# Reading x first and summing the first conditioning blocks on TensorE in a hybrid decoder layer

## The chip, the cores and the metric

The kernel runs on one core of one Trainium2 chip. The metric is the device time of one execution in microseconds. It covers the whole layer: all weights are read from HBM in float32, and all products are formed on the chip.

## What is computed

One decoder layer on 512 tokens of width 2048. A conditioning vector `c` gives six modulation vectors; the first two of them (shift and scale of the mixer's norm) are what the change concerns. Cut to that part, the reference is:

```python
c_act = jax.nn.silu(c)
mod = c_act @ w_ada[l] + b_ada[l]                  # 2048 x 12288 weights
sh_m, sc_m, gt_m, sh_f, sc_f, gt_f = jnp.split(mod[:, None, :], 6, axis=-1)
h = rmsnorm(x, pre_mix_norm[l]) * (1.0 + sc_m) + sh_m
proj = h @ w_in[l]                                 # 512 x 2048 by 2048 x 8208
o_hg = hgrn2_group(proj[..., :HG_COLS], ...)       # gated recurrences, chunks of 64
o_gdn = gdn_group(proj[..., HG_COLS:], ...)
y = concatenate([o_hg, o_gdn]) @ w_out[l]
x = x + gt_m * rmsnorm(y, post_mix_norm[l])
h = rmsnorm(x, pre_ffn_norm[l]) * (1.0 + sc_f) + sh_f
y = square(relu(h @ w_ff1[l])) @ w_ff2[l]
x = x + gt_f * rmsnorm(y, post_ffn_norm[l])
```

## The kernel before, in words

**Stages.** The program has a start stage, a mixer stage, an output projection and a feed-forward stage. In all of them a float32 product is formed as three matmuls of rounded parts (`mm3`): high part by high part, high by low, low by high. ScalarE makes the high part of a weight tile (L197) and VectorE (sometimes Pool) the low part (L199).

**The start stage.** The model width of 2048 is cut into 16 blocks of 128 rows, here called blocks 0 to 15 (`kt`). For each block the stage needs a scale and a shift vector of 128 numbers. Each is a sum over the 2048 entries of `c_act`, times a column of `w_ada`. The needed part of `w_ada` (33.5 MB) is packed as 128 tiles of 128 x 512 (256 KB), two to a slot: one of the scale, one of the shift. `GROUPS` says which blocks share a slot: before, blocks 0 and 1 are groups by themselves (four slots each), and the other blocks go in pairs (eight slots each). There are 64 slots.

A slot's tile holds, for w = 128 columns, four row sets side by side; for w = 256, two. `ada_vector` (L440) multiplies each row set by one entry of `c_act` per partition and adds it to a sum, one VectorE pass a row set. `ada_pool` does the same for the shift tile: ScalarE scales the row sets in place (L449), and Pool adds the whole tile to a sum of 128 x 512 (L451). In group 0 VectorE does both tiles (`NV = 1`). When a group's slots are through, TensorE sums over the partitions by `column_sum` (ones as the moving operand, two matmuls of 64 columns each), and VectorE forms the scale `sc1` and shift `shm` (L845 to L847).

**The norm of x.** x is loaded in eight transfers of 512 KB (L798), after the first four slots (`X_AT = 4`). ScalarE squares each half row block and sums it (L633), VectorE and Pool form the reciprocal root (L426, L427: a `pow` on Pool), TensorE spreads it over the partitions (`spread`), and VectorE copies it into `R1`.

**From blocks to matmuls.** `mod_thread` takes the groups in order. For each block it transposes x on TensorE (L342; block 0 beforehand), multiplies by scale and `R1` on VectorE (L858, `ht`), and writes the high part `hH` (ScalarE) and the low part `hL` (VectorE L863; from block 4 on, for even blocks, Pool L868). A token ("mod", block) then releases the matmuls of that block. `CUTS` orders these as units of eight weight tiles: `(first block, number of blocks, from, to)` over the list of 16 column blocks (two heads of each kind). A unit of two blocks covers four column blocks, a unit of four covers two. The first five column blocks accumulate in PSUM banks of their own; the others are partial sums that VectorE adds into SBUF after each unit (L705).

**What sets the order.** In the start stage the queues of TensorE, ScalarE and SyncE are written out in the order of a small planner (`run`). It keeps a modelled clock: each matmul costs its modelled time, each load 0.73 or 1.46 us on a modelled DMA clock (`on_load`), a thread yields the time that it means to wait, and while all threads wait, the next projection matmuls are emitted (`fill_thread`). The planner does not model VectorE or Pool; their order is the framework's. `AHEAD = 7` slots are loaded ahead. The slot tiles rotate over 14 tiles that are not yet otherwise used and `NADA` more. A weight tile is loaded three units ahead.

**Masks.** `masks` builds on Pool the constant masks for the later recurrences, one of six steps for each group that `mod_thread` begins.

Of the kernel before, what the change touches and what calls it, by code (L numbers as in the profile page):

```python
# [8 lines left out]
F32 = mybir.dt.float32  # L9
# [4 lines left out]
ALU = mybir.AluOpType  # L14

P = 128
NADA = 2
ADV = 0.17
LP0 = 7
LP1 = 23  # L20
# [1 line left out]
LATE = 20  # L22
AHEAD = 7
X_IN = 3.0
X_AT = 4
W_AT2 = 8
W_AT = 4
NLAST = 5
SLACK = 1.57
SLACK1 = 1.0  # L30
NV = 1
PJ = 3
LOOK = 6
T = 512
D = 2048
KT = D // P
# [10 lines left out]
    ("g", 0, (C_GQ, C_GK, C_GV, C_GG)), ("g", 1, (C_GQ, C_GK, C_GV, C_GG)),  # L47
    ("h", 0, (C_HF, C_HQ, C_HI, C_HG)), ("h", 1, (C_HF, C_HQ, C_HI, C_HG))))
START_BLOCKS = G0 + H0 + G1 + H1
CUTS = [(0, 2, 0, 16), (2, 2, 0, 16), (4, 2, 0, 8), (6, 2, 0, 8), (4, 4, 8, 16),  # L50
        (8, 4, 0, 8), (12, 4, 0, 8), (8, 4, 8, 16), (12, 4, 8, 16)]
START_UNITS = [(k0, nk, START_BLOCKS[i : i + 8 // nk])
               for k0, nk, lo, hi in CUTS for i in range(lo, hi, 8 // nk)]
IN1_COLS = [cc + h * P for h in range(2, NH) for cc in (C_GK, C_GQ, C_GV, C_HF, C_HQ, C_HI, C_GG, C_HG)]

GROUPS = [(0,), (1,)] + [(k, k + 1) for k in range(2, KT, 2)]
SLOTS = [(g, j) for g, kts in enumerate(GROUPS) for j in range(4 * len(kts))]
ADA_REST = (4, 3, 2, 5)


def by_tiles(name, a):

    import numpy as np

    if name == "w_ada":
        w = a[0].reshape(P, KT, -1)
        out = []
        for g, j in SLOTS:
            n = len(GROUPS[g]) * P
            nr = 512 // n  # L70
            for seg in (1, 0):
                c0 = seg * D + GROUPS[g][0] * P
                out.append(w[:, nr * j : nr * (j + 1), c0 : c0 + n].reshape(P, 512))
        for seg in ADA_REST:
            for cb in range(4):
                for r in range(KT):
                    out.append(w[:, r, seg * D + cb * 512 : seg * D + (cb + 1) * 512])
        return np.stack(out)
    if name == "w_in":
        w = a[0].reshape(KT, P, -1).transpose(1, 0, 2)  # L80
        out = []
        for k0, nk, bls in START_UNITS:
            out.append(np.concatenate([w[:, k0 : k0 + nk, cc + h * P : cc + (h + 1) * P] for _, h, cc in bls], 1))
        for col in IN1_COLS:
            for hf in range(2):
                out.append(w[:, 8 * hf : 8 * (hf + 1), col : col + P])
        return np.concatenate([t.reshape(-1) for t in out] + [w[:, :, C_AB : C_AB + 16].reshape(-1)])
    if name == "w_ff1":
        return a[0].reshape(4, 4, P, DFF // 256, 256).transpose(3, 0, 2, 1, 4).reshape(-1, P, 1024)
    if name in ("w_out", "w_ff2"):  # L90
        return a[0].reshape(-1, 2, P, 4, 512).transpose(0, 3, 2, 1, 4).reshape(-1, P, 1024)
    return a
# [143 lines left out]
def hybrid_layer_kernel(  # L236
# [7 lines left out]
    nc = tc.nc  # L244
    PSUM = bass.MemoryType.PSUM
    xf = x[0]
# [105 lines left out]
    ones = const.tile([P, P], F32, name="ones")  # L352
# [3 lines left out]
    mhalf = const.tile([P, 16], F32, name="mhalf")  # L356
# [49 lines left out]
    c2 = const.tile([P, KT], F32, name="c2")  # L406
# [14 lines left out]
    tl = const.tile([P, NCH, NH], F32, name="tl")  # L421
    fold = const.tile([32, 16], F32, name="fold")

    def rsqrt_to(dst, src, scale, eps):
        n = src.shape[1]
        nc.vector.tensor_scalar(out=dst, in0=src, scalar1=scale, scalar2=eps, op0=ALU.mult, op1=ALU.add)  # L426
        nc.gpsimd.tensor_tensor(out=dst, in0=dst, in1=mhalf[:, :n], op=ALU.pow)  # L427

    def ada_load(alloc, seg, cb, r):
        a = alloc(f"ada{seg}_{cb}_{r}")  # L430
# [3 lines left out]
    def ada_vector(a, ncol, r0, nr, acc, first):  # L434
        for r in range(nr):
            av, cv = a[:, r * ncol : (r + 1) * ncol], c2[:, r0 + r : r0 + r + 1]
            if first and r == 0:
                nc.vector.tensor_scalar(out=acc, in0=av, scalar1=cv, scalar2=None, op0=ALU.mult)
            else:
                nc.vector.scalar_tensor_tensor(out=acc, in0=av, scalar=cv, in1=acc, op0=ALU.mult, op1=ALU.add)  # L440
# [12 lines left out]
    def column_sum(ps, i, a, w, start=True, stop=True):  # L453
        for g in range(2):
            s = slice(64 * g, 64 * (g + 1))
            mm(ps[s, i, : w.shape[1]], a[:, s], w, start, stop, cost=0.08)
# [91 lines left out]
    def sm(name):  # L548
        return bank("wh", name)
# [215 lines left out]
    def on_load(us):  # L765
        dma[0] = max(dma[0], clock[0]) + us
# [16 lines left out]
    xarr = []  # L783
    masking = masks()

    def ada_thread():
        nl = 0
        for i, (g, j) in enumerate(SLOTS):
            w = len(GROUPS[g]) * P
            nr = 512 // w  # L790
            while nl < min(len(SLOTS), i + 1 + AHEAD):
                ada_slot(nl)
                nl += 1
                if nl == X_AT:
                    for tok in range(4):
                        for hf in range(2):
                            hs = slice(hf * 1024, (hf + 1) * 1024)
                            nc.sync.dma_start(out=xn4[:, tok, hs], in_=xf[tok * P : (tok + 1) * P, hs])  # L798
                            on_load(1.46)
                            xarr.append(dma[0])  # L800
                    tokens.add(("xload", 0))
                if nl == W_AT:
                    ws._load()
                if nl == LATE:
                    late_loads()
                if nl == W_AT2:
                    for _ in range(2):
                        ws._load()
            at, t = arrive.pop(i)
            yield max(0.0, at + (ADV if g > 0 else 1.0) - clock[0])  # L810
            if j == 0:
                sums[g] = [sp.tile([P, n], F32, tag=f"asum{n}", name=f"asum{n}_{g}", bufs=2)
                           for n in (256, 512)]
            ada_vector(t[0], w, nr * j, nr, sums[g][0][:, :w], j == 0)
            if g < NV:
                ada_vector(t[1], w, nr * j, nr, sums[g][1][:, :w], j == 0)
            else:
                ada_pool(t[1], w, nr * j, nr, sums[g][1], j == 0)
            if j == 4 * len(GROUPS[g]) - 1:
                tokens.add(("ada", g))  # L820
# [5 lines left out]
    def mod_thread():  # L826
        for g, kts in enumerate(GROUPS):
            w = len(kts) * P
            if g > 0:
                next(masking, None)  # L830
            if g == 3:
                late_consts()
            yield "ada", g
            yield 2.0 if g else 0.5
            n = len(kts)
            asc, ash = sums.pop(g)
            pc = sm(f"pc{g}").rearrange("p (k n) -> p k n", n=64)
            nr = 1 if g < NV else 512 // w
            for i in range(n):
                column_sum(pc, i, asc[:, i * P : (i + 1) * P], ones[:, :64])  # L840
                for r in range(nr):
                    column_sum(pc, n + i, ash[:, r * w + i * P : r * w + (i + 1) * P], ones[:, :64],
                               r == 0, r == nr - 1)
            ks = slice(kts[0], kts[0] + n)
            nc.vector.tensor_tensor(out=sc1[:, ks], in0=pc[:, 0:n, 0], in1=b_scm[:, ks], op=ALU.add)  # L845
            nc.vector.tensor_tensor(out=sc1[:, ks], in0=sc1[:, ks], in1=w_pm[:, ks], op=ALU.mult)
            nc.vector.tensor_tensor(out=shm[:, ks], in0=pc[:, n : 2 * n, 0], in1=b_shm[:, ks], op=ALU.add)  # L847
            if g == 0:
                yield "x", 0
            for kt in kts:  # L850
                if kt in early:
                    ps = early[kt]
                else:
                    yield 0.5
                    ps = sm(f"pt{kt}")
                    x_transposes(ps, kt)
                ht = mt("ht", f"ht{kt}", 2)
                nc.vector.scalar_tensor_tensor(out=ht, in0=ps, scalar=sc1[:, kt : kt + 1], in1=R1,  # L858
                                               op0=ALU.mult, op1=ALU.mult)
                yield 0.0  # L860
                if kt < 4 or kt % 2:
                    nc.scalar.activation(out=hH[:, kt, :], in_=ht, func=AF.Identity, bias=shm[:, kt : kt + 1])
                    nc.vector.scalar_tensor_tensor(out=hL[:, kt, :], in0=ht, scalar=shm[:, kt : kt + 1],  # L863
                                                   in1=hH[:, kt, :].bitcast(F32), op0=ALU.add, op1=ALU.subtract)
                else:
                    nc.scalar.activation(out=ht, in_=ht, func=AF.Identity, bias=shm[:, kt : kt + 1])
                    nc.scalar.copy(out=hH[:, kt, :], in_=ht)
                    nc.gpsimd.tensor_tensor(out=hL[:, kt, :], in0=ht, in1=hH[:, kt, :].bitcast(F32),  # L868
                                            op=ALU.subtract)
                yield 1.0  # L870
                tokens.add(("mod", kt))
        yield from decay_terms()
# [931 lines left out]
```

## Time and profile before

| | |
|---|---|
| Median of three runs | 2583.98 us (2583.64 to 2587.78) |
| The profiled execution | 2583.66 us, span in the profile 2581.9 us, mean granted clock 0.986 |
| TensorE busy, whole span | 96% |
| VectorE, ScalarE, Pool busy, whole span | 73%, 43%, 40% |
| DMA, whole span | 350.64 MB, mean 136 GB/s |
| First main matmul of the projection | 27.43 us |
| Scale of the last group of blocks formed | 196.06 us |

The span runs from the first to the last recorded instruction; the time also has what lies around it (1.8 us in the profiled execution). A stretch in the view of busy time by stretches begins with its bounds and length in us; then come the busy times of TensorE's matmuls (PE), its weight loads (PEld), VectorE (DVE), ScalarE (ACT) and Pool with their instruction counts in brackets, the clock granted to TensorE, the share of DMA time and the GB/s. A row without a certain engine means that the engine had nothing in that selection. A row of the chain of waits names the waiting engine and line, what it waited for, the total in us, how often, and the longest. A row of groups has busy time and the mean of one in ns, and then idle time before it. A row of the timeline has its start, its length, and its engine, line and tiles; several equal instructions in sequence are merged (x20).

### The profile page before, as it was taken

What the parts mean: (1) busy time and instruction counts of PE and PEld (TensorE: products, weight loads), DVE (VectorE), ACT (ScalarE), POOL (GpSimd) and SP (SyncE); (2) the same over time, 40 slices, a digit from 0 to 9 for tenths busy, and PEclk for the clock granted to TensorE, in tenths of its full rate; (3) what the DMA queues carried; (4) which work ended last, traced back from release to release, by engine and by line L of the source; (5) the groups of instructions that cost most, each with busy time, mean ns of one, the idle gap of its engine ahead of it and who ended that gap; (6) DMA issues with size and microseconds to landing.
All of it is one profiled execution on the core that took longest, in us unless ns stands there. A gap on an engine that the chain in (4) does not pass through costs nothing.

```text
span 2581.9 us, 34110 instructions
## 1 busy us (share of the span) xinstructions
PE 2469.1 (96%) x12627; PEld 2007.2 (78%) x12627; DVE 1875.9 (73%) x2709; ACT 1118.1 (43%) x1765; POOL 1032.4 (40%) x646
## 2 busy tenths in 40 slices
PE   5889999998999899999999999999999999999998
PEld 3667777777777778788788888888888888888876
DVE  7997877768586765634668776777768777677787
ACT  5553544544444452423444444444434434443333
POOL 5561344445444440000244535445354444533333
PEclk9999999999999999999999999999999999999999
DMA  8762434444545432344423332433424333232334
GB/s 320 255 203 74 128 119 147 139 148 138 160 142 164 139 115 82 130 140 155 154 98 133 104 135 95 146 123 106 142 95 139 110 127 135 94 114 82 122 116 161
DMA packets 127300, 350.64 MB, mean 136 GB/s; under 512 B 14247, under 2 KB 18713, under 8 KB 125981
## 3 DMA queue, kind: packets, MB, share of 16 engines
q1 hardware_dynamic: 126938, 348.41, 40.0%
q8 instruction: 99, 1.62, 0.3%
q14 instruction: 67, 0.55, 0.1%
q10 hardware_dynamic: 196, 0.06, 0.0%
HBM read 340.01 MB, written 8.40 MB: 135 GB/s over the span
## 4 chain that ended last, share of the span: by engine, by line
PE 67%; DVE 6%; POOL 1%; ACT 1%; issue 1%; DMA 1%; DVEq 0%; ACTq 0%; POOLq 0%
PE pf L331 27%; PE pg L331 22%; PE pj L331 9%; PE pout L331 7%; DVE wl L199 1%; DVE uc L1034 1%; PE pa L331 1%; DVE utmp L1032 1%; POOL y L1728 0%; POOL aacc L451 0%; PE p L331 0%; DVE x2r L1746 0%; DMA ada<-in_w_ada_dram 0%; DVE zkT L493 0%; PE pz L331 0%
## 5 line engine op out<-in xcount | busy, mean ns | idle before, releaser
L199 DVE TENSOR_TENSOR wl<-raw,wh 128x1024 fp32r<-128x1024 f32 x506 | 720.1, 1424 | 427.8 <-ACT wh L197 422.6
L197 ACT CAST wh<-raw 128x1024 fp32r<-128x1024 f32 x512 | 538.0, 1052 | 943.4 <-PE pf L331 285.9
L165 POOL TENSOR_TENSOR raw<-raw,raw 128x1024 f32<-128x1024 f32 x150 | 438.9, 2941 | 392.7 <-DMA raw<-in_w_ff_dram 181.6
L331 PE MATMUL pf<-h2L,wh 128*128 128x512 f32 x1024 | 399.9, 391 | 0.0
L331 PE MATMUL pf<-h2H,wh 128*128 128x512 f32 x1024 | 399.7, 390 | 0.0
L331 PE MATMUL pf<-h2H,wl 128*128 128x512 f32 x1024 | 399.6, 390 | 0.0
L451 POOL TENSOR_TENSOR aacc<-ada,aacc 128x512 f32<-128x512 f32 x180 | 268.9, 1494 | 253.5 <-ACT ada L449 242.2
L331 PE MATMUL pg<-wl,cH 128*128 128x512 f32 x840 | 327.6, 390 | 1.1 <-DVE wl L199 1.1
L331 PE MATMUL pg<-wh,cL 128*128 128x512 f32 x840 | 327.3, 390 | 0.0
L331 PE MATMUL pg<-wh,cH 128*128 128x512 f32 x840 | 327.3, 390 | 0.0
L331 PE MATMUL pj<-hH,wh 128*128 128x512 f32 x768 | 325.2, 423 | 0.0
L331 PE MATMUL pj<-hH,wl 128*128 128x512 f32 x768 | 305.0, 397 | 4.4 <-DVE wl L199 4.4
L331 PE MATMUL pj<-hL,wh 128*128 128x512 f32 x768 | 304.0, 396 | 0.0
L331 PEld LDWEIGHTS pf<-h2H,wh 128*128 128x128 f32 x1024 | 192.7, 188 | 39.7
L331 PEld LDWEIGHTS pf<-h2L,wh 128*128 128x128 f32 x1024 | 192.7, 188 | 39.6
L331 PEld LDWEIGHTS pf<-h2H,wl 128*128 128x128 f32 x1024 | 192.7, 188 | 39.6
L451 POOL TENSOR_TENSOR gacc<-ada,gacc 128x512 f32<-128x512 f32 x64 | 108.4, 1694 | 278.9 <-ACT ada L449 278.9
L1627 DVE TENSOR_TENSOR y<-pg,y 128x512 f32<-128x512 f32 x344 | 219.0, 682 | 0.0
L331 PEld LDWEIGHTS pg<-wl,cH 128*128 128x128 f32 x840 | 157.8, 188 | 35.0 <-DVE wl L199 2.3
L331 PEld LDWEIGHTS pg<-wh,cH 128*128 128x128 f32 x840 | 157.8, 188 | 32.7
L331 PEld LDWEIGHTS pg<-wh,cL 128*128 128x128 f32 x840 | 157.8, 188 | 32.5
L331 PEld LDWEIGHTS pj<-hH,wl 128*128 128x128 f32 x768 | 146.4, 191 | 39.2 <-DVE wl L199 6.5
(434 smaller groups left out, 3770.3 us busy)
## 6 DMA issues: line engine op xcount, KB each, us to landing
raw<-in_w_ff_dram SPq DMA_DIRECT2D x256, 512.0 KB, 4.0
raw<-in_w_in_dram SPq DMA_DIRECT2D x128, 512.0 KB, 3.4
ada<-in_w_ada_dram SPq DMA_DIRECT2D x256, 256.0 KB, 3.4
adas<-in_w_ada_dram SPq DMA_DIRECT2D x128, 256.0 KB, 4.4
raw<-in_w_out_dram SPq DMA_DIRECT2D x40, 512.0 KB, 3.5
xo<-in_x_dram SPq DMA_DIRECT2D x8, 512.0 KB, 9.4
xr<-in_x_dram SPq DMA_DIRECT2D x8, 512.0 KB, 6.8
x2d<-z SPq DMA_DIRECT2D x4, 1024.0 KB, 5.7
```

The costliest lines, as they stand in the source:

```text
L165: self.nc.gpsimd.tensor_tensor(out=out, in0=ra, in1=rb, op=op)
L197: self.cast = self.nc.scalar.copy(out=h, in_=raw).ins
L199: eng.tensor_tensor(out=lo, in0=raw, in1=h.bitcast(F32), op=ALU.subtract)
L331: nc.tensor.matmul(ps, lhsT=lhsT, rhs=rhs, start=start, stop=stop)
L451: nc.gpsimd.tensor_tensor(out=acc, in0=a, in1=acc, op=ALU.add)
L1032: nc.vector.tensor_tensor(out=tmp[:, :, :n], in0=xj, in1=uc[:, :, j : j + 1].broadcast_to([P, NCH, n]), op=ALU.mult)
L1034: nc.vector.tensor_tensor(out=uc[:, :, j + 1 :], in0=uc[:, :, j + 1 :], in1=tmp[:, :, :n], op=ALU.subtract)
L1627: nc.vector.tensor_tensor(out=dst, in0=ps, in1=dst, op=ALU.add)
```

## The change

- `x_loads` puts the eight transfers of x ahead of all slots on SyncE's queue.
- For groups 0 and 1 (`PEG = 2`) TensorE forms the sums: the 128 x 128 row set is the stationary operand, one column of `c_act` the moving one. 16 such matmuls accumulate one vector, 64 in all, into one PSUM bank (`pcp`). The tiles of these groups are ordered scale first, then shift (`slot_tiles`). The column sums of these groups are gone.
- Blocks 4 to 15 come in three groups of four with w = 512: a slot's tile is one row set, one VectorE pass, one ScalarE pass, and the Pool sum needs no further folding by `column_sum`. The sums of these groups live in the tiles of the later stage's pool.
- `CUTS` takes blocks 4 to 7 of the first eight column blocks as one set of units of four, as it already did for the others.
- `NADA` goes from 2 to 4, so 18 tiles rotate instead of 16.
- The masks are made two steps at a time, and on Pool not before the last `pow` of the norm.

```diff
-NADA = 2
+NADA = 4
-X_AT = 4
+PEG = 2
-NV = 1
-CUTS = [(0, 2, 0, 16), (2, 2, 0, 16), (4, 2, 0, 8), (6, 2, 0, 8), (4, 4, 8, 16),
+CUTS = [(0, 2, 0, 16), (2, 2, 0, 16), (4, 4, 0, 8), (4, 4, 8, 16),
         (8, 4, 0, 8), (12, 4, 0, 8), (8, 4, 8, 16), (12, 4, 8, 16)]
-GROUPS = [(0,), (1,)] + [(k, k + 1) for k in range(2, KT, 2)]
+GROUPS = [(0,), (1,), (2, 3)] + [tuple(range(k, k + 4)) for k in range(4, KT, 4)]
+def slot_tiles(g, j):
+    if g < PEG:
+        return [(1 - j // 2, 2 * (j % 2) + k) for k in range(2)]
+    return [(1, j), (0, j)]
...
-        nc.gpsimd.tensor_tensor(out=dst, in0=dst, in1=mhalf[:, :n], op=ALU.pow)
+        last_pow.append(nc.gpsimd.tensor_tensor(out=dst, in0=dst, in1=mhalf[:, :n], op=ALU.pow).ins)
...
     def ada_thread():
         nl = 0
+        x_loads()
...
-                if nl == X_AT:
-                    (the eight loads of x)
...
-            ada_vector(t[0], w, nr * j, nr, sums[g][0][:, :w], j == 0)
-            if g < NV:
-                ada_vector(t[1], w, nr * j, nr, sums[g][1][:, :w], j == 0)
+            if g < PEG:
+                if i == 0:
+                    sums["pe"] = sm("pcp").rearrange("p (k n) -> p k n", n=1)
+                for (seg, jj), a in zip(slot_tiles(g, j), t):
+                    for r in range(4):
+                        mm(sums["pe"][:, 2 * g + 1 - seg, :], a[:, r * P : (r + 1) * P],
+                           c2[:, 4 * jj + r : 4 * jj + r + 1], 4 * jj + r == 0, 4 * jj + r == KT - 1, cost=0.11)
             else:
+                if j == 0:
+                    sums[g] = [ada_pool_.tile([P, T], F32, tag="ada", bufs=LOOK + 1, name=f"asum{k}_{g}")
+                               for k in range(2)]
+                ada_vector(t[0], w, nr * j, nr, sums[g][0][:, :w], j == 0)
                 ada_pool(t[1], w, nr * j, nr, sums[g][1], j == 0)
...
             if g > 0:
-                next(masking, None)
+                with tc.issue_after(last_pow[-1]):
+                    for _ in range(2):
+                        next(masking, None)
...
-            nr = 1 if g < NV else 512 // w
+            if g < PEG:
+                pc = sums["pe"][:, 2 * g : 2 * g + 2, :]
+            else:
+                (column sums as before, with nr = 512 // w)
```

More of the change, by code (lines that the diff above doesn't have):

```diff
@@ L70, in by_tiles @@
             nr = 512 // n
-            for seg in (1, 0):
+            for seg, jj in slot_tiles(g, j):
                 c0 = seg * D + GROUPS[g][0] * P
-                out.append(w[:, nr * j : nr * (j + 1), c0 : c0 + n].reshape(P, 512))
+                out.append(w[:, nr * jj : nr * (jj + 1), c0 : c0 + n].reshape(P, 512))
         for seg in ADA_REST:
@@ L422, in hybrid_layer_kernel @@
     fold = const.tile([32, 16], F32, name="fold")
+    last_pow = []
     def rsqrt_to(dst, src, scale, eps):
@@ L784, in hybrid_layer_kernel, with x_loads @@
     masking = masks()
+    def x_loads():
+        for tok in range(4):
+            for hf in range(2):
+                hs = slice(hf * 1024, (hf + 1) * 1024)
+                nc.sync.dma_start(out=xn4[:, tok, hs], in_=xf[tok * P : (tok + 1) * P, hs])
+                on_load(1.46)
+                xarr.append(dma[0])
+        tokens.add(("xload", 0))
     def ada_thread():
         nl = 0
+        x_loads()
         for i, (g, j) in enumerate(SLOTS):
@@ L793, in ada_thread @@
                 nl += 1
-                if nl == X_AT:
[L795 to L801, printed above, removed]
                 if nl == W_AT:
@@ L810, in ada_thread @@
             yield max(0.0, at + (ADV if g > 0 else 1.0) - clock[0])
-            if j == 0:
-                sums[g] = [sp.tile([P, n], F32, tag=f"asum{n}", name=f"asum{n}_{g}", bufs=2)
-                           for n in (256, 512)]
-            ada_vector(t[0], w, nr * j, nr, sums[g][0][:, :w], j == 0)
-            if g < NV:
-                ada_vector(t[1], w, nr * j, nr, sums[g][1][:, :w], j == 0)
-            else:
+            if g < PEG:
[5 more added lines that the diff above has]
+                           c2[:, 4 * jj + r : 4 * jj + r + 1], 4 * jj + r == 0, 4 * jj + r == KT - 1, cost=0.11)
+            else:
+                if j == 0:
+                    sums[g] = [ada_pool_.tile([P, T], F32, tag="ada", bufs=LOOK + 1, name=f"asum{k}_{g}")
+                               for k in range(2)]
+                ada_vector(t[0], w, nr * j, nr, sums[g][0][:, :w], j == 0)
                 ada_pool(t[1], w, nr * j, nr, sums[g][1], j == 0)
@@ L835, in mod_thread @@
             n = len(kts)
-            asc, ash = sums.pop(g)
-            pc = sm(f"pc{g}").rearrange("p (k n) -> p k n", n=64)
-            nr = 1 if g < NV else 512 // w
[L839 to L843, printed above, removed]
+            if g < PEG:
+                pc = sums["pe"][:, 2 * g : 2 * g + 2, :]
+            else:
+                asc, ash = sums.pop(g)
+                pc = sm(f"pc{g}").rearrange("p (k n) -> p k n", n=64)
+                nr = 512 // w
+                for i in range(n):
+                    column_sum(pc, i, asc[:, i * P : (i + 1) * P], ones[:, :64])
+                    for r in range(nr):
+                        column_sum(pc, n + i, ash[:, r * w + i * P : r * w + (i + 1) * P], ones[:, :64],
+                                   r == 0, r == nr - 1)
             ks = slice(kts[0], kts[0] + n)
```

## The prediction

> **What bounds the kernel now.** I read the page's summary first, then busy time by stretches, the chains of waits, the groups by form, and single rows of the timeline. The change touches only the first 210 us, where the conditioning of the pre-norm is summed tile by tile (128 tiles of `w_ada`, 64 slots of two) and the input projection's first sixteen column blocks run beside it.
>
> ```profile
> span 2581.9 us, 34110 instructions
> 62.00:107.00 45.00, 36.44 (x191) 27.48 (x191) 41.98 (x61) 22.06 (x45) 24.61 (x17) 0.96 0.76 268
> 107.00:152.00 45.00, 37.70 (x191) 29.32 (x190) 41.47 (x59) 22.03 (x43) 27.74 (x18) 0.89 0.72 244
> 152.00:200.00 48.00, 42.02 (x221) 33.06 (x220) 43.31 (x55) 22.61 (x42) 28.75 (x19) 0.93 0.52 167
> 200.00:260.00 60.00, 59.42 (x349) 45.40 (x348) 44.86 (x94) 24.30 (x46) 6.14 (x9) 1.00 0.24 75
> 20.00:30.00 10.00, 4.15 (x10) 2.37 (x10) 6.26 (x16) 7.22 (x16) 2.47 (x3) 1.00 1.04 397
> ```
>
> The busy columns are PE, PEld, DVE, ACT, POOL, then granted clock, DMA share, GB/s. From 62 to 200 us VectorE (DVE) is busy over 90% and TensorE idles 8 us in 45 at a reduced clock; from 200 on TensorE is full (59.42 of 60). So what TensorE gets done earlier before 200 reaches the end of the span. DMA is the limit only until about 40 us (397 GB/s from 20 to 30).
>
> ```profile
> PE pc L331 <- DVE asum L440: 10.3, 4, 5.9
> PE pph L331 <- DVE parth L705: 3.7, 1, 3.7
> SPq L778 <- POOL asum L451: 52.3, 26, 6.6
> SPq L778 <- DVE asum L440: 24.5, 23, 3.0
> POOL asum L451 <- ACT adas L449: 43.5, 13, 9.2
> ACT wh L197 <- PE pph L331: 12.8, 3, 5.4
> L440 DVE SCALAR_TENSOR_TENSOR asum<-adas,c,asum 128x256 f32<-128x256 f32 x105 | 88.4, 842 | 2.0
> L440 DVE SCALAR_TENSOR_TENSOR asum<-adas,c,asum 128x128 f32<-128x128 f32 x45 | 16.9, 413 | 0.5
> L451 POOL TENSOR_TENSOR asum<-adas,asum 128x512 f32<-128x512 f32 x52 | 76.9, 1481 | 45.7 <-ACT adas L449 43.5
> L858 DVE SCALAR_TENSOR_TENSOR ht<-pt,sc,R 128x512 f32<-128x512 f32 x16 | 12.0, 748 | 6.2 <-PE pt L342 6.1
> ```
>
> TensorE waits for the summed tiles; the DMA queue waits for their buffers (52.3 and 24.5 us), which the sums free; Pool's adds wait for ScalarE. The sums, not the transfers, set the pace.
>
> **How even that pace is.** The first add of each finished group's scale stands here:
>
> ```profile
> 39.74 0.15 DVE L845 TENSOR_TENSOR sc<-pc,vecT 128x1 f32<-128x1 f32 x1
> 63.20 0.15 DVE L845 TENSOR_TENSOR sc<-pc,vecT 128x2 f32<-128x2 f32 x1
> 107.19 0.15 DVE L845 TENSOR_TENSOR sc<-pc,vecT 128x2 f32<-128x2 f32 x1
> 196.06 0.15 DVE L845 TENSOR_TENSOR sc<-pc,vecT 128x2 f32<-128x2 f32 x1
> 105.12 1.86 POOL L451 TENSOR_TENSOR asum<-adas,asum 128x512 f32<-128x512 f32 x1 [7.23 <-ACT adas L449]
> 105.75 1.51 DVE L440 SCALAR_TENSOR_TENSOR asum<-adas,c,asum 128x256 f32<-128x256 f32 x1
> 107.45 0.48 DVE L440 SCALAR_TENSOR_TENSOR asum<-adas,c,asum 128x256 f32<-128x256 f32 x1
> ```
>
> Eight slots take 23.5 us (39.74 to 63.20); sixteen take 44.0 (63.20 to 107.19), and the 32 after them 88.9: 2.75 us a slot throughout. A pass of 256 columns takes 0.48 us free and 1.51 beside a Pool add. The Trainium skill (SBUF — State Buffer, section "Who interferes with whom") says that a VectorE instruction with two SBUF inputs and a GpSimd instruction reading SBUF exclude each other; the 0.48 against 1.51 agrees.
>
> **The change, part by part.** The tail ahead of the first matmul, and its warm and cold pitch:
>
> ```profile
> 10.43 0.22 ACT L600 ACTIVATE e<-e 128x16 f32<-128x16 f32 x1 [1.14 <-DVE e L599]
> 12.77 1.06 ACT L633 ACTIVATE junkx<-xo 128x1024 bf16<-128x1024 f32 x1 [2.13 <-DMA xo<-in_x_dram]
> 25.88 0.74 DVE L858 SCALAR_TENSOR_TENSOR ht<-pt,sc,R 128x512 f32<-128x512 f32 x1
> 27.43 0.79 PE L331 MATMUL accg<-hH,wh 128*128 128x512 f32 x1 [1.99 <-ACT hH L862]
> 42.79 0.80 PE L331 MATMUL accg<-hH,wh 128*128 128x512 f32 x1 [1.60 <-ACT hH L862]
> 37.01 1.33 PE L331 MATMUL pc<-ones,asum 128*64 128x64 f32 x20 [3.54 <-DVE asum L440]
> 85.02 0.63 PE L331 MATMUL ppg<-hL,wh 128*128 128x512 f32 x1
> 85.45 0.63 PE L331 MATMUL ppg<-hH,wl 128*128 128x512 f32 x1
> 88.28 0.39 PE L331 MATMUL ppg<-hH,wh 128*128 128x512 f32 x1
> 88.51 0.39 PE L331 MATMUL ppg<-hL,wh 128*128 128x512 f32 x1
> 85.87 1.05 PE L342 MATMUL pt<-ident,xo 128*128 128x128 f32 x4
> ```
>
> 1. *x first.* ScalarE could begin the squares at 10.65 (end of the Exp) and begins at 12.77, waiting for x: 2.1 us at most come back. On SyncE's queue the eight x transfers move past group 0's eight tiles; the bytes ahead of the first matmul are the same, and what follows keeps its order.
>
> 2. *TensorE sums groups 0 and 1.* VectorE loses 48 passes of 128 columns (0.41 each, 19.8 us), Pool three adds, ScalarE their scalings. TensorE gains 64 matmuls with one output column. None is in the trace; the nearest row is the column sums, 20 instructions in 1.33 us, 0.067 each, two to a call. Weights here are twice as wide. That row lies at half clock (TensorE had idled 3.54 us), so a call at twice the width costs at most 0.27, and no less than these 0.13 at full clock; I take 0.2, the middle, as the clock is rising there. The Trainium skill (TensorE: Matmul & The Clock Gate, section "LDWEIGHTS (loading the stationary operand)") gives columns/1.2 ns, an estimate of 0.21 a call; no row here shows it. By the written order's clock, 24 of group 0's 32 calls stand behind the broadcast of the last row block, so about 4.8 us follow it, against the 2.1 gained: first matmul near 29.5 instead of 27.43. Group 1 then costs 32 calls (6.4 us) and the twelve matmuls of block 0 instead of VectorE's passes: block 1's first matmul near 41 instead of 42.79.
>
> 3. *Group 2.* ScalarE's queue holds its scalings behind block 1's `hH`, so Pool's adds start near 41, but VectorE's passes, freed of group 1, are done as tiles land. I expect group 2 complete near 53 instead of 63.20: ten earlier, the main early gain. Bounds: 47 (as tiles land) and 63.
>
> 4. *Rows of 512 columns.* Two passes of 256 (0.48 each, issued 0.51 apart) become one near 0.75 (the 128x512 pass of 748 ns): 0.25 saved a slot, 4 us in sixteen slots. So group 3 (blocks 4 to 7) is complete at 53 + 44 - 4 = 93. Bounds: 85 and 103.
>
> 5. *Fours.* Block 4 no longer comes after eight of those slots but after all sixteen. TensorE has blocks 0 to 3 until about 88 and then starves; the four blocks come some 2.7 us apart, the last near 105. The first waiting unit has two column blocks, six matmuls per block of rows. That is some 12 us idle, and the clock falls. In exchange, blocks 5 to 7's partial sums need three fewer adds.
>
> 6. *From 105 on.* Of `hL`'s matmuls (one in three), the trace has:
>
> ```profile
> 0.00:107.00 107.00, 28.96 (x69) 14.04 (x69) 4.14 (x5) 1.28 (x1) 0.94 0.84 297
> 107.00:210.00 103.00, 45.20 (x110) 20.88 (x110) 7.63 (x5) 6.49 (x5) 0.92 0.57 190
> 200.00:210.00 10.00, 7.59 (x32) 3.47 (x32) 0.58 (x1) 1.00 0.17 52
> ```
>
> There are 256 such (16 blocks x 16), so 187 are left at 107; 110 less the 16 of the decay terms (half of the x32 row) run until 210, leaving 93. In the new order 24 of the last twelve blocks' 576 matmuls are done at 105, so 184 are left: about where the old kernel stands at 107. To reach 93 takes 91 x 3 = 273 matmuls at 0.228 (88.28 to 88.51), 62.2 us; decay terms 7.6; eight sets of transposes at 0.6, 4.8; two fours of column sums, 64 instructions near 0.053, 3.4; cold restart 2.5 (0.43 apart at 85.02 and 85.45); stalls on partial adds 5; waits at the two later sums 2. Sum 87.5: reached at 192.5 instead of 210, because TensorE now always has four blocks of backlog where it waited before. Gain 17.5 us.
>
> 7. *Masks later.* About 12 us of Pool work moves from 2-16 us to after the last pow, where Pool waits for ScalarE anyway (43.5 us in all). Cover gone, up to 3 us of delay to group 2; I take 0. *Deeper rings* (18 tiles for 16): the buffer waits shorten, inside the pace above.
>
> The profiled run took 2583.66 us (1.8 outside the span), the median of the runs is 2583.98. 2583.66 - 17.5 = 2566.
>
> **The rivals.** *The wider pass saves nothing.* If each pass of 512 hides wholly under a Pool add, as 105.75 under 105.12, the slot stays at 2.75 us: group 3 at 97, block 7 at 109 and some 2 us lost again at a later sum, so 6 to 7 us less gain: 2573. Against it: 107.45 shows half the passes free. The Trainium skill's exclusion rule (as above) is this rival's.
>
> *No starving.* If sixteen slots run as freely as the tiles land (16.8 MB of `w_ada`, x and weights, some 27 MB at 397 GB/s, 68 us after the start-up), block 4 is there at 85, block 7 at 96: 9 us more, 2557.
>
> *The wait for four takes it back.* If group 3 comes at 103 to 110, block 7 comes at 115 to 122 and the gain is 0 to 7: no change. For it: the DMA and ACT queues are written in one order, and ScalarE's casts wait for TensorE (12.8 us).
>
> *Slower.* One mechanism: ScalarE's last scalings of the sixteen stand behind a weight cast whose buffer is freed only after TensorE's stalled matmuls on partial adds, so the slot rises to 4 us instead of 2.75. Sixteen slots are then 20 us longer, block 7 at 125, and the time about 2586 to 2594. It decides from block 7 at 123 on. Against it: 2.75 us held over 56 slots with the same coupling.
>
> **How the numbers follow.** Forecast 0.40 (2559 to 2572, its own range); wider pass worthless 0.14; no starving 0.13; wait takes it back 0.18; slower 0.15. A measurement tells 0.2%, 5 us, from no change. Faster: 0.40 + 0.14 + 0.13 = 0.67; same 0.18; slower 0.15. The range 2553 to 2591 leaves out the ends of the third and last cases.
>
> **What would show it.** The first main matmul within 2 us of 29; group 2's scale near 53; group 3's near 93, then a TensorE gap of about 10 us ahead of block 4 and a half clock there; no gaps over 3 us after 110; passes of 512 columns near 0.75 us where Pool is idle. It is wrong if group 3 comes after 103, if the one-column matmuls take over 0.3 us a call, or if TensorE waits for group 4 or 5.

## The result and the profile after

The changed kernel takes 2593.28 us (median of seven, 2591.04 to 2596.14) against 2584.97 us before (seven, 2583.35 to 2587.78): a ratio of 1.0032 with a 95% interval of 1.0020 to 1.0044. It is 8.3 us slower; the forecast was 2566, 18 us faster. The profiled execution took 2592.62 us, its span is 2590.9.

Busy time by stretches of the kernel after, and the first stretch of the kernel before (PE, PEld, DVE, ACT, POOL, clock, DMA, GB/s):

```profile
span 2590.9 us, 34014 instructions
25.00:62.00 37.00, 34.84 (x136) 31.05 (x136) 13.35 (x22) 6.80 (x13) 8.36 (x28) 1.00 0.67 234
62.00:107.00 45.00, 40.23 (x186) 30.44 (x185) 40.90 (x46) 26.75 (x45) 28.58 (x20) 0.96 0.82 290
107.00:152.00 45.00, 35.81 (x148) 25.85 (x147) 29.55 (x34) 16.86 (x24) 27.47 (x18) 0.73 0.68 227
152.00:200.00 48.00, 43.10 (x241) 34.01 (x240) 42.90 (x43) 21.56 (x30) 39.93 (x24) 0.96 0.58 202
200.00:260.00 60.00, 59.69 (x330) 46.05 (x330) 39.94 (x74) 26.93 (x49) 7.93 (x10) 1.00 0.22 75
```

```profile
25.00:62.00 37.00, 26.75 (x131) 20.08 (x130) 34.16 (x52) 22.90 (x52) 15.41 (x11) 0.86 0.87 311
```

The two kernels part in the first row. From 25 to 62 us TensorE is busier than before (34.84 of 37 against 26.75), and everything else does much less: VectorE 13.35 against 34.16, ScalarE 6.80 against 22.90, the DMA share 0.67 against 0.87. A part of that is meant, since the passes for groups 0 and 1 are gone from VectorE and ScalarE; the waits below are not. From 62 on TensorE is as busy as before or busier, apart from 107 to 152, where it waits for blocks 4 to 7 at a granted clock of 0.73 (35.81 of 45 against 37.70).

Single rows of the kernel after show how one engine stops the next:

```profile
17.00 3.54 PE L337 MATMUL pcp<-c,adas 128*128 128x1 f32 x16
20.97 10.24 PE L337 MATMUL pcp<-c,adas 128*128 128x1 f32 x48
34.96 0.77 PE L337 MATMUL accg<-hH,wh 128*128 128x512 f32 x1
35.53 0.63 PE L337 MATMUL accg<-hL,wh 128*128 128x512 f32 x1
35.96 0.63 PE L337 MATMUL accg<-hH,wl 128*128 128x512 f32 x1
36.39 3.41 PE L337 MATMUL pcp<-c,adas 128*128 128x1 f32 x16
49.22 0.16 DVE L865 TENSOR_TENSOR sc<-pcp,vecT 128x1 f32<-128x1 f32 x1 [15.03 <-PE pcp L337]
52.34 0.72 ACT L882 ACTIVATE hH<-ht,shm 128x512 fp32r<-128x512 f32 x1 [18.27 <-DVE ht L878]
54.02 0.35 DVE L446 TENSOR_SCALAR asum<-adas,c 128x256 f32<-128x256 f32 x1
54.80 2.70 POOL L459 TENSOR_TENSOR asum<-adas,asum 128x512 f32<-128x512 f32 x2 [24.00 <-ACT adas L457]
53.12 0.79 PE L337 MATMUL accg<-hH,wh 128*128 128x512 f32 x1 [1.60 <-ACT hH L882]
58.87 0.39 PE L337 MATMUL acch<-hH,wh 128*128 128x512 f32 x1
73.27 0.16 DVE L865 TENSOR_TENSOR sc<-pc,vecT 128x2 f32<-128x2 f32 x1
112.60 0.16 DVE L865 TENSOR_TENSOR sc<-pc,vecT 128x4 f32<-128x4 f32 x1 [0.86 <-PE pc L337]
197.78 0.16 DVE L865 TENSOR_TENSOR sc<-pc,vecT 128x4 f32<-128x4 f32 x1 [3.81 <-PE pc L337]
```

The one-column matmuls (`pcp`) come 0.213 us apart (48 in 10.24), two to a call: 0.43 us a call, 27 us for the 64. Then the brackets lead down the chain: VectorE stands 15.03 us at block 1's scale, because its queue is in order and that sum is not through TensorE; ScalarE stands 18.27 us for VectorE's `ht`; Pool stands 24.00 us for ScalarE's scalings of group 2, which are queued behind that `hH`. Only from 53 on is group 2 worked on at all; VectorE's first pass for it is at 54.02. Its scale comes at 73.27, against 63.20 before.

The clock column says 1.00 from 25 to 62, but the pitch says otherwise: main matmuls are 0.43 us apart at 35.53 and 35.96, and their length falls from 0.63 to 0.39 only at 58.87. Where the two differ, the pitch (the time from one start to the next) is read here, and "slow pace" and "fast pace" mean 0.43 and 0.23 us for 512 columns.

### The profile page after: what moved, and what is told of

Same layout as the page of the kernel before. It is cut to its first block, busy times and chain, and to the rows that moved or that the text cites. A ratio compares the mean times of both kernels' runs of the same rounds, so it can differ in the third digit from the quotient of the medians.

```text
span 2590.9 us, 34014 instructions
## 1 busy us (share of the span) xinstructions
PE 2496.1 (96%) x12679; PEld 2032.0 (78%) x12679; DVE 1841.9 (71%) x2601; ACT 1104.5 (43%) x1701; POOL 1038.7 (40%) x646
## 4 chain that ended last, share of the span: by engine, by line
PE 68%; DVE 5%; POOL 1%; ACT 1%; issue 1%; DMA 0%; DVEq 0%; SPq 0%; ACTq 0%; POOLq 0%
PE pf L337 27%; PE pg L337 22%; PE pj L337 9%; PE pout L337 7%; DVE wl L205 1%; PE pa L337 1%; DVE uc L1054 1%; DVE utmp L1052 1%; POOL y L1748 0%; PE p L337 0%; DVE x2r L1766 0%; DVE zkT L501 0%; PE py L337 0%; PE pz L337 0%; PE pm L1539 0%
```

## The experiments

"Of before" means that the edit is made to the kernel before, "of after" to the kernel after. The kernel before measured 2585.2 to 2585.8 us beside them. All ratios are to it, with 95% intervals.

### Taking the TensorE sums out, and putting them in alone

`e_no_pe`, of after: `PEG = 2` becomes 0, and VectorE, ScalarE and Pool sum groups 0 and 1 again.

```diff
-PEG = 2
+PEG = 0
+NV = 1
...
+                if g < NV:
+                    ada_vector(t[1], w, nr * j, nr, sums[g][1][:, :w], j == 0)
+                else:
                     ada_pool(t[1], w, nr * j, nr, sums[g][1], j == 0)
```

> The changed kernel with groups 0 and 1 summed as before (VectorE, ScalarE, Pool); x first, fours, masks later and the longer ring stay. Theory A (the 64 one-column calls at 0.43 us stand in TensorE's queue ahead of blocks 0 and 1 and hold the clock at half): block 1's first matmul comes back from 53 to about 43 us, and the time falls by 8 to 15 us, to 2578 to 2585. Theory B (the wait for four at block 4 costs it): block 4 still starts near 114, TensorE still crawls for 20 us behind it, and the time stays at 2589 to 2594.

`e_pe_only`, of before: groups 0 and 1 as in the kernel after (`PEG`, `slot_tiles`, `pcp`), nothing else.

> The kernel before, with only the sums of groups 0 and 1 moved to TensorE; x where it was, pairs, old masks. Theory A: block 1's first matmul near 50 to 53 instead of 42.8, group 2's scale 8 to 10 us later than 63.2, and 6 to 12 us slower than before (2591 to 2597). Theory B: the later pace makes up for it, within 4 us of before (2581 to 2589).

`e_no_pe` took 2584.90 us, ratio 0.9994 (0.9985 to 1.0003): 8.4 us less than the kernel after. `e_pe_only` took 2601.16, ratio 1.0059 (1.0045 to 1.0072): 15.4 us more than the kernel before. Rows of `e_no_pe`, then of `e_pe_only`:

```profile
32.90 0.80 PE L338 MATMUL accg<-hH,wh 128*128 128x512 f32 x1 [2.39 <-ACT hH L886]
47.03 0.80 PE L338 MATMUL accg<-hH,wh 128*128 128x512 f32 x1 [1.60 <-ACT hH L886]
67.28 0.15 DVE L869 TENSOR_TENSOR sc<-pc,vecT 128x2 f32<-128x2 f32 x1
190.36 0.16 DVE L869 TENSOR_TENSOR sc<-pc,vecT 128x4 f32<-128x4 f32 x1 [4.85 <-PE pc L338]
```

```profile
38.04 0.77 PE L338 MATMUL accg<-hH,wh 128*128 128x512 f32 x1
```

Block 1 enters at 47.03 instead of 53.12, group 2 is complete at 67.28 instead of 73.27. The TensorE sums cost time in both surroundings. Taken alone, they put block 0's first matmul at 38.04, block 1's at 52.78 and group 2's scale at 74.22, about where theory A had them; the time is above its range (2591 to 2597), so the price of that delay was still put too low.

### Half of them, wider ones, and others between them

`e_pe_half`, of after, leaves half of the products out:

```diff
-                    for r in range(4):
+                    for r in (0, 3):
```

> The changed kernel with every second of the 64 one-column calls left out (half of the products of groups 0 and 1 are left out). Theory A (the price of a call, 0.43 us, times their number): block 1's first matmul 10 to 13 us earlier than 53.1, and the time falls to about that of the kernel without them, 2583 to 2588. Theory B (their place in the written order, not their number): block 1 stays after 50 and the time at 2590 to 2594.

It took 2585.10 us, ratio 0.9996 (0.9988 to 1.0005).

```profile
20.65 5.12 PE L337 MATMUL pcp<-c,adas 128*128 128x1 f32 x24
40.59 0.16 DVE L865 TENSOR_TENSOR sc<-pcp,vecT 128x1 f32<-128x1 f32 x1 [11.77 <-PE pcp L337]
43.59 0.80 PE L337 MATMUL accg<-hH,wh 128*128 128x512 f32 x1 [1.60 <-ACT hH L882]
44.49 0.35 DVE L446 TENSOR_SCALAR asum<-adas,c 128x256 f32<-128x256 f32 x1
64.73 0.16 DVE L865 TENSOR_TENSOR sc<-pc,vecT 128x2 f32<-128x2 f32 x1
```

The price of an instruction stays (24 in 5.12, 0.213 each), block 1 comes at 43.59, and the time is that of no such sums at all: what costs is the length of the string on TensorE, and half of it adds nothing.

This run also stands in for the prediction's own price: 32 calls at 0.43 us are 13.7 us on TensorE, where 64 at 0.2 were forecast as 12.8. It takes 2585.10 us and not 2566, so the price explains 8.2 of the 27.3 us by which the forecast missed. VectorE still waits 11.77 us for block 1's sum, and group 2's scale comes 20 us after its first pass (44.49 to 64.73), at 64.73 where 53 was forecast.

`e_pe_64`, of after, moves 64 equal columns instead of one:

```diff
-c2[:, 4 * jj + r : 4 * jj + r + 1], ...
+c2[:, 4 * jj + r : 4 * jj + r + 1].broadcast_to([P, 64]), ...
```

(`pcp` gets 64 columns for each vector.)

> The changed kernel with 64 equal moving columns instead of one in the sums: the same weight loads, more columns streamed. If the clock stayed at half because one column counts for no activity: the clock rises after a few us of sums, a call falls towards 0.2 us, and block 1's first matmul comes near 42 to 46 instead of 53.1, time 2584 to 2589. If weight loads alone set price and clock: 0.43 a call and block 1 at 53 as before, time 2591 to 2596.

It took 2593.38 us, ratio 1.0030 (1.0019 to 1.0041), the time of the kernel after.

```profile
21.44 10.34 PE L337 MATMUL pcp<-c,adas 128*128 128x64 f32 x48
53.70 0.79 PE L337 MATMUL accg<-hH,wh 128*128 128x512 f32 x1 [1.60 <-ACT hH L882]
```

48 in 10.34 against 48 in 10.24: the columns moved are not what is paid for. That leaves what one column and 64 have in common, loading 128 x 128 numbers as weights twice a call. The column sums before also move 64 columns, at 0.067 an instruction; their weights are 64 columns wide instead of 128. And the weight loads are busy 31.05 of 37 us in the first row of the profile after.

`e_pe_warm`, of after, puts a matmul of 512 columns on constants behind each call, to see whether the pace rises with more columns in between:

```diff
+                        nc.tensor.matmul(accs[START_BLOCKS[4]].rearrange("p (a n) -> p a n", a=4), lhsT=onesr,
+                                         rhs=onesr.unsqueeze(1).broadcast_to([P, 4, P]), start=True, stop=True)
```

> The changed kernel with one matmul of 512 columns on constants behind each of the 64 one-column calls (its result is not used). If the half clock sets the price and dense columns raise it: after some 5 us the call and its filler come every 0.45 to 0.55 us, the call itself near 0.25, and the clock is full by 30 us. If weight loads cost the same at any clock: 0.43 and 0.23, 0.66 a pair. If the clock doesn't rise: 0.43 and 0.43, 0.86 a pair. Block 1 is later than 53 in the last two cases.

It took 2617.54 us in its one run.

```profile
72.84 0.42 PE L337 MATMUL pcp<-c,adas 128*128 128x1 f32 x2
73.12 0.77 PE L828 MATMUL acch<-onesr 128*128 128x512 f32 x1
73.69 0.42 PE L337 MATMUL pcp<-c,adas 128*128 128x1 f32 x2
```

A call and its filler take 0.85 us (72.84 to 73.69), as they did at 60, and the filler is at its slow length (0.77). The pace does not rise in some 60 us. So the price at the fast pace remains unmeasured. (Block 1 enters only at 81.88 here; the long time is that of the added matmuls.)

### The groups of four alone

`e_fours_only`, of before: `GROUPS` and `CUTS` of the kernel after, the sums in the later stage's tiles, the masks two steps at a time but not held back. TensorE sums, x and the rings stay as before.

```diff
-CUTS = [(0, 2, 0, 16), (2, 2, 0, 16), (4, 2, 0, 8), (6, 2, 0, 8), (4, 4, 8, 16),
+CUTS = [(0, 2, 0, 16), (2, 2, 0, 16), (4, 4, 0, 8), (4, 4, 8, 16),
-GROUPS = [(0,), (1,)] + [(k, k + 1) for k in range(2, KT, 2)]
+GROUPS = [(0,), (1,), (2, 3)] + [tuple(range(k, k + 4)) for k in range(4, KT, 4)]
```

> The kernel before, with only the groups of four, the wider passes and the new units (masks two at a time, but not held back). Theory A: starving at block 4 and the backlog after it nearly cancel: 2576 to 2585, 0 to 8 us faster than before. Theory B: block 4 to 7 come 20 us late and little is won back: 2589 to 2595.

It took 2579.53 us (2577.55 to 2581.48), ratio 0.9975 (0.9965 to 0.9985): 6.2 us less than the kernel before beside it (2585.76), and the fastest of all that ran.

```profile
62.90 0.15 DVE L846 TENSOR_TENSOR sc<-pc,vecT 128x2 f32<-128x2 f32 x1
98.71 0.16 DVE L846 TENSOR_TENSOR sc<-pc,vecT 128x4 f32<-128x4 f32 x1 [0.67 <-PE pc L331]
115.59 0.75 DVE L859 SCALAR_TENSOR_TENSOR ht<-pt,sc,R 128x512 f32<-128x512 f32 x1 [2.57 <-PE pt L342]
183.02 0.16 DVE L846 TENSOR_TENSOR sc<-pc,vecT 128x4 f32<-128x4 f32 x1 [3.91 <-PE pc L331]
```

From group 2 to the last group, 48 slots take 120.1 us (62.90 to 183.02), against 132.9 before (63.20 to 196.06): 0.27 us saved a slot in the mean. It is not even: the sixteen slots of blocks 4 to 7 save 8.2 us (35.8 against 44.0), the 32 after them 4.6 (84.3 against 88.9), 0.14 a slot. The four blocks enter at the end of their sixteen slots, the last one (block 7) at 115.59.

`e_fours_pairs` is `e_fours_only` with the old `CUTS`:

```diff
-CUTS = [(0, 2, 0, 16), (2, 2, 0, 16), (4, 4, 0, 8), (4, 4, 8, 16),
+CUTS = [(0, 2, 0, 16), (2, 2, 0, 16), (4, 2, 0, 8), (6, 2, 0, 8), (4, 4, 8, 16),
```

> The kernel with fours alone, but blocks 4 to 7 of the first eight column blocks in units of two blocks and four columns, so that twelve matmuls instead of six stand behind each new block. If TensorE starves there for lack of work per block: 2 to 4 us faster than the fours alone (2579.5), 2574 to 2578. If the chain from transpose to low part sets the time whatever work there is: 2578 to 2582.

2581.62 us, ratio 0.9983 (0.9974 to 0.9992): 2 us more than `e_fours_only` and still faster than before. More matmuls behind each new block don't help, as the second reading had it.

`e_fours_late`, of before, keeps pairs up to block 7, the old `CUTS` and the masks' pace of one step, and has fours from block 8, with the sums in the later stage's tiles:

```diff
+GROUPS = [(0,), (1,)] + [(k, k + 1) for k in range(2, 8, 2)] + [tuple(range(k, k + 4)) for k in range(8, KT, 4)]
```

> The kernel before, with pairs up to block 7 and fours of 512 columns only for blocks 8 to 15, where TensorE has a backlog. If fours win by backlog and wider passes and lose only by starving at block 4: 2572 to 2580, with no TensorE gap over 3 us after 110. If wider passes and fours win nothing: 2583 to 2587.

2597.25 us, ratio 1.0043 (1.0030 to 1.0055). This missed by 20 us. Its busy time by stretches:

```profile
152.00:200.00 48.00, 38.64 (x186) 29.81 (x186) 39.53 (x35) 20.01 (x28) 32.88 (x20) 0.93 0.47 156
200.00:260.00 60.00, 52.63 (x266) 38.07 (x265) 35.25 (x65) 23.98 (x45) 7.07 (x9) 0.94 0.17 58
```

TensorE idles 9.4 of the 48 us before 200, where the kernel after idles 4.9, and 7.4 of the 60 after it, where that one idles 0.3: work runs out while the last four blocks are formed and enter. My expectation looked at the sums alone. `e_fours_pairs` has the same units and differs from this kernel only in the group of four for blocks 4 to 7 and in the masks' pace, and it is 15.6 us faster. The masks are through by 16.2 us here, so it is the group of four for blocks 4 to 7 that is missing, and not the units. Why it matters so much was not shown. The 32 slots of blocks 8 to 15 take 84.2 us here (110.05 to 194.26) against 88.9 before: fours with the wider pass save 0.15 us a slot there.

### x first and the masks

`e_x_first`, of before, moves only the loads of x to the front:

```diff
+        x_loads()
...
-                if nl == X_AT:
-                    (the eight loads of x)
```

> The kernel before, with only x loaded ahead of the slots. Theory A (group 0's tiles land last and its 32 VectorE passes then follow them): first main matmul near 32 to 33 us instead of 27.4, as in the kernel without the TensorE sums, block 1's near 47, and 3 to 7 us slower than before (2588 to 2593). Theory B (the masks held back or the longer ring are what costs in that kernel): within 2 us of before.

`e_x_masks` adds to it that the masks are made two steps at a time after the last pow:

```diff
-                next(masking, None)
+                with tc.issue_after(last_pow[-1]):
+                    for _ in range(2):
+                        next(masking, None)
```

> The kernel before, with x first and the masks held back behind the last pow (two steps at a time). With x first alone, Pool's pow of the second row block stood behind the masks and block 0 came at 39.8 us. If that queue is the whole of it: block 0 near 33, as in the kernel with all but the TensorE sums, and 4 to 7 us gained on x first alone (2596): 2588 to 2592, still slower than before, because group 0's passes now follow x. If the masks don't matter: 2594 to 2597.

`e_x_first` took 2596.09 us, ratio 1.0040 (1.0026 to 1.0054); `e_x_masks` 2588.69, ratio 1.0013 (1.0004 to 1.0021). Rows of the first, then of the second:

```profile
21.75 0.56 POOL L427 TENSOR_TENSOR rstdx<-rstdx,mhalf 128x1 f32<-128x1 f32 x1
22.69 0.80 PE L331 MATMUL prx<-dgx,ones 128*128 128x128 f32 x2 [9.42 <-DVE dgx L641]
39.80 0.80 PE L331 MATMUL accg<-hH,wh 128*128 128x512 f32 x1 [2.39 <-ACT hH L864]
```

```profile
32.12 0.80 PE L331 MATMUL accg<-hH,wh 128*128 128x512 f32 x1 [2.39 <-ACT hH L868]
```

With x first alone, the pow runs on Pool right behind a mask, without idle time ahead of it (no bracket in its row); TensorE waits 9.42 us and block 0 enters at 39.80, where 32 to 33 was expected; the masks ahead of the pow were left out of that expectation, and the time is above its range too. With the masks held back it enters at 32.12, still 4.7 later than before (27.43), and the kernel is 7.4 us faster than with x first alone, but slower than before. Holding the masks back is what makes x first bearable here; it does not make it pay.

`e_fours_ring` is `e_fours_only` with the masks held back and `NADA = 4`:

```diff
-NADA = 2
+NADA = 4
...
+                with tc.issue_after(last_pow[-1]):
                     for _ in range(2):
                         next(masking, None)
```

> The fours alone, plus the masks held back and the ring of 18 tiles; x where it was. If these two are neutral where x isn't first: 2577 to 2582, as the fours alone (2579.5). If the masks now take Pool from group 1 or 2, or the ring changes the written order for the worse: 2584 to 2588, which would explain the 2585 of the kernel without the TensorE sums without x.

2583.71 us, ratio 0.9994 (0.9985 to 1.0003): 4.2 us more. Pool's first add of group 1 in `e_fours_only`, then that of `e_fours_ring` with group 1's scale:

```profile
29.75 1.57 POOL L451 TENSOR_TENSOR asum<-adas,asum 128x512 f32<-128x512 f32 x1 [4.36 <-ACT adas L449]
```

```profile
39.72 3.94 POOL L453 TENSOR_TENSOR asum<-adas,asum 128x512 f32<-128x512 f32 x3
44.89 0.16 DVE L849 TENSOR_TENSOR sc<-pc,vecT 128x1 f32<-128x1 f32 x1 [7.72 <-PE pc L331]
```

Where Pool sums group 1, masks held back stand in front of that sum: 29.75 becomes 39.72. In the kernel after Pool has no such sum; it idles from 30.8 to 54.8, so the masks stand in front of nothing. `e_no_pe` has the sum again, behind the masks (its first add of group 1 is at 37.68), so the 8.4 us probably understate the price of the TensorE sums. The ring was not taken apart from the masks. From `e_fours_ring` to `e_no_pe` only x first is added, and both have the ratio 0.9994 to before: no price of x first shows there.

### Releasing four blocks at once

`e_fours_tok` is `e_fours_only` with the tokens of blocks 4 to 7 given only when all four are formed:

```diff
-                tokens.add(("mod", kt))
+                if g != 3:
+                    tokens.add(("mod", kt))
+            if g == 3:
+                for kt in kts:
+                    tokens.add(("mod", kt))
```

> The fours alone, but blocks 4 to 7 are released together, so that the next block's transposes don't stand in TensorE's queue behind the matmuls that wait for this block's low part. If that in-turn chain (5.1 us a block) is what starves TensorE: the four ht come 2 to 3 us apart, block 7 some 5 us earlier, and 2 to 4 us are gained: 2575 to 2578. If the work per block on VectorE, ScalarE and Pool sets it: 5 us apart as now, 2579 to 2583.

2583.93 us, ratio 0.9994 (0.9985 to 1.0003): 4.4 us slower than `e_fours_only`. Blocks 4 and 7 in it, its last scale, and two rows of its chain of waits:

```profile
100.24 0.75 DVE L859 SCALAR_TENSOR_TENSOR ht<-pt,sc,R 128x512 f32<-128x512 f32 x1
106.19 0.75 DVE L859 SCALAR_TENSOR_TENSOR ht<-pt,sc,R 128x512 f32<-128x512 f32 x1 [0.22 <-PE pt L342]
179.73 0.16 DVE L846 TENSOR_TENSOR sc<-pc,vecT 128x4 f32<-128x4 f32 x1 [0.15 <-PE pc L331]
```

```profile
PE pph L331 <- DVE wl L199: 5.3, 2, 3.5
PE acch L331 <- POOL wl L199: 2.7, 1, 2.7
```

The four come 2.0 us apart instead of some 5, so the mechanism was there, block 7 is 9.4 us earlier, and nothing is gained; 2 to 4 us were expected. In these two rows TensorE waits 8 us for low parts of weights (`wl`), against 0.8 in `e_fours_only` in the same stretch (100 to 210 us). Whether these waits are all of the loss was not settled.

## Why the prediction was wrong, step by step

*What failed, in short.* Step 2 put a call at half its price, which is 8.2 of the 27.3 us missed (`e_pe_half`). Step 3 had group 2 complete 20 us too soon, 12 of them at the forecast price as well. Step 6 turned an early block 7 into time, and the kernels with an early block 7 did not gain it.

*Step 2, the price of a call.* The prediction took 0.2 us a call within 0.13 to 0.27; it is 0.43 at the pace that prevailed. The row that I scaled, the column sums at 37.01 (20 instructions in 1.33 us), has 64 columns of weights an instruction, and doubling it to 128 was the error: 0.213 is 3.2 times 0.067. The row of transposes in the same fence, at 85.87 (four of 128 columns in 1.05 us, issued while matmuls were 0.43 apart), gives 0.2 to 0.26 an instruction and was the nearer one. The figure of the Trainium skill (TensorE: Matmul & The Clock Gate, section "LDWEIGHTS (loading the stationary operand)") that I set beside it, 0.107 an instruction for 128 columns, is half of the 0.213 measured at the slow pace. I also let the pace rise; it did not. (Four transposes take 1.05 at the slow pace and 0.60, step 6's own figure, at the fast one, so the pace bears on the price.) So the 64 calls are 27 us on TensorE, not 13: first main matmul 34.96 (forecast 29.5), block 1's 53.12 (forecast 41).

*Step 3 failed with it.* "VectorE's passes, freed of group 1, are done as tiles land" forgot that VectorE's queue holds block 1's scale ahead of group 2's passes. The 15.03 us row is that wait. And it gave the eight slots 12 us, from 41 to 53, where they took 19 from VectorE's first pass (54.02 to 73.27), 2.4 a slot. Group 2 came at 73.27; forecast 53, with an upper bound of 63. With half the calls it is 64.73, so this step fails at the forecast price too.

*Step 4 was right in the mean.* The forecast was 0.25 us saved a slot; `e_fours_only` shows 0.27. That is partly luck: by groups it is 0.51 for blocks 4 to 7 and 0.14 after them, and `e_fours_late` shows 0.15 for fours from block 8 on. The rival that the wider pass saves nothing is refuted; why the first sixteen slots gain more stays open. In the kernel after, by form:

```profile
L448 DVE SCALAR_TENSOR_TENSOR asum<-adas,c,asum 128x512 f32<-128x512 f32 x45 | 54.1, 1203 | 0.4
```

A pass of 512 has a mean of 1203 ns beside Pool's adds, against two of 842 before.

*Step 5 was too low.* Blocks 4 and 7 of the kernel after:

```profile
113.82 0.75 DVE L878 SCALAR_TENSOR_TENSOR ht<-pt,sc,R 128x512 f32<-128x512 f32 x1 [0.20 <-PE pt L348]
130.09 0.75 DVE L878 SCALAR_TENSOR_TENSOR ht<-pt,sc,R 128x512 f32<-128x512 f32 x1 [3.47 <-PE pt L348]
```

They are 5.4 us apart, not 2.7: the next block's transposes stand in TensorE's queue behind matmuls that wait for the last block's `hL` (in `e_fours_tok`, without that order, they are 2.0 apart). From 112.60 (forecast 93) to block 7 it is 17.5 us, where 12 were forecast.

*Step 6: its gain did not come.* Its sum gives 17.5 us gained with block 7 at 105, so no gain at 122.5. Block 7 at 130.09 makes 2591.3 by that line; the profiled execution took 2592.62. `e_fours_only`, with block 7 at 115.59, makes 2576.8; its profiled execution took 2578.22. So far the line holds. But `e_fours_pairs` has block 7 at 111.39, which makes 2573, and took 2584; `e_fours_tok` has it at 106.19, about where the forecast wanted it, which makes 2567, and took 2583. The line fails just where the forecast needed it. Another reading covers more of the kernels: the last group's scale and the span.

| Kernel | last scale | span | between |
|---|---|---|---|
| before | 196.06 | 2581.9 | 2385.8 |
| after | 197.78 | 2590.9 | 2393.1 |
| `e_fours_only` | 183.02 | 2576.1 | 2393.1 |
| `e_no_pe` | 190.36 | 2584.2 | 2393.8 |
| `e_fours_tok` | 179.73 | 2581.2 | 2401.5 |
| `e_fours_late` | 194.26 | 2596.2 | 2401.9 |

`after`, `e_fours_only` and `e_no_pe`, with the same groups and units, end 2393 us after the last sum, 7.3 later than before; so do `e_pe_half`, `e_pe_64` and `e_fours_ring` (2392.6 to 2393.3). `e_x_first` and `e_x_masks`, with the old groups, lie at 2386.1 and 2385.8, as before. `e_pe_only` breaks the pattern: old groups, and 2392.6. So fours are worth 13.0 us at the last sum and cost 7.3 behind it, and the backlog that I counted on doesn't shorten what follows the last sum. In the kernel after, the last scale is even 1.7 us behind the old one: the 13 us saved in the sums are spent again, 10.4 of them by group 2 (73.27 against 62.90 in `e_fours_only`), and what remains is the 7.3. That the tail is longer because the last block follows the sum by 8.9 us (206.64) and not by 3.5 (199.60) is my reading and covers 5.3 of it. `e_fours_tok` and `e_fours_late` end 8 us later still. In `e_fours_late` the last block follows by 15.0 (209.31), which would cover most of it; in `e_fours_tok` it follows by 8.9, and its delay stays open, as that of `e_pe_only` does.

*Step 1* took the Exp on ScalarE as the limit of the squares; they were put ahead of it:

```profile
5.04 1.06 ACT L641 ACTIVATE junkx<-xo 128x1024 bf16<-128x1024 f32 x1 [0.40 <-DMA xo<-in_x_dram]
```

They begin 7.7 us earlier than before (12.77), not 2.1, but group 0's tiles now come behind x, and without the TensorE sums block 0 enters at 32.90 (`e_no_pe`). *Step 7* was right for this kernel: Pool idles 24.00 us behind the masks. Its bound of 3 us of delay to group 2 with the cover gone was too low: in `e_fours_ring`, with the longer ring, group 2's scale is at 66.77, 3.9 later than in `e_fours_only`.

*The rivals.* The slower one forecast 2586 to 2594 from block 7 at 123 on, and that is where the time lies. That is luck: its mechanism, slots of 4 us, is not what happened, for the slots took 2.46 (73.27 to 112.60). `e_pe_half` comes close to the third rival, a wait for four that takes the gain back: group 3 at 106.25 (103 to 110 there), block 7 at 124.04, and no change of the time. A string on TensorE that holds VectorE, ScalarE and Pool one behind the other was not among the rivals.

## What to carry to other kernels

Work that is moved to an idle engine is priced by the row with the same size of weights, and at the pace that the engine will have there; here a factor of two in one price cost 8 us. Then ask which in-order queues stand behind its result: the 27 us of matmuls stopped VectorE for 15, ScalarE for 18 and Pool for 24, while with half as many the time is that without them (2585.10 against 2584.90). A gain that is to come from a milestone reached early has to be followed to the end: block 7 came at 106.19 in one kernel, and nothing was gained. A change of several parts should be run part by part: the groups of four alone are faster (0.9975), and what was added to them took more than they gave.

## What the runs showed of the hardware

- A float32 matmul with 128 x 128 weights and one moving column is two instructions of 0.213 us each at the slow pace; with 64 columns it costs the same (10.24 against 10.34 us for 48).
- Such matmuls did not raise TensorE's pace, though TensorE was busy nearly throughout from 17 to 50 us: the main matmuls between them stayed 0.43 us apart, and the fast pace came at 58.87, some 5.7 us into the dense matmuls from 53.12. With a matmul of 512 columns behind each, the pace was still the slow one at 73. The Trainium skill (TensorE: Matmul & The Clock Gate, section "What's actually happening") has the clock rise after about 3.4 us of sustained busy time; busy time in the profile's sense was not enough here to bring the fast pace.
- The clock column read 1.00 in stretches where the pitch was the slow one (25 to 62 us of the kernel after), so whether the clock or something else held the pace is not shown.
